# Weight pieces split 80 places further ahead in the scheduler's priority

## The chip, the cores and the metric

The kernel runs as one program on one core of a Trainium2 chip. The metric is device time in microseconds (us) of one execution, lower is better. Every number below comes from timed runs or from one execution recorded by the hardware profiler. Engines are named as the profile names them: PE (TensorE, matmuls), PEld (TensorE's weight loads), DVE (VectorE), ACT (ScalarE), POOL (GpSimd), SP (SyncE, which issues most transfers).

## The reference, cut to what matters

Two models of two layers each run one after the other on 256 tokens of width 1024, in float32. The first has an even layer (an mLSTM branch and a sparse-attention branch, "nsa", beside each other) and an odd layer (HGRN2, a gated linear recurrence). The second has, per layer, a mixer (pooling in layer 0, a gated unit "SGU" in layer 1) and an MLP, with gains and shifts that come from a conditioning vector ("ada").

```
x = x + even_layer(rms_norm(x) ...)       # mLSTM || nsa, then @ ev_w_out
x = x + hgrn2_layer(rms_norm(x) ...)      # then @ od_w_out
for i in range(2):
    mod = silu(c) @ ada_w[i] + ada_b[i]   # six vectors of 1024
    x = x + g1 * mixer_i(modulate(rmsnorm(x), sh1, sc1))
    x = x + g2 * (square(relu(modulate(rmsnorm(x), sh2, sc2) @ w1[i])) @ w2[i])
```

Most of the work is products of 256 tokens with large weight matrices.

## The kernel before, in words

**Weights.** Every large matrix is read in loads of 128 x 2048 numbers (1 MB) into one of three "raw" buffers (`load_raw`, line 150, issued by SP). A load holds two pieces of 128 x 1024. To keep float32 accuracy on the faster matmul form, a piece w is split into two parts (`split_w`, line 155): ACT copies w into a rounded buffer `whi` (line 161), DVE subtracts and writes the rest into `wlo` (line 162). There are four buffers of each. The activations are split in the same way into `ahi` and `alo` (or `ghl` for the MLP's hidden values). A product is then three matmuls per 128 x 128 block: whi with ahi, whi with alo, wlo with ahi (lines 221 to 223; lines 206 to 208 where the tokens are the stationary side; lines 1057 and 1058 in the MLP's second product, where one matmul takes ahi and alo together).

One piece makes one output tile: 24 matmuls for a piece of 8 blocks (`tile_T`), 12 or 24 in `tiles_tok`, 16 in the MLP's second product, where four pieces make one output tile. `Weights.piece` (line 181) asks for the load of a raw buffer when its first piece comes, and calls `split_w` just ahead of the tile's matmuls. The very first piece is split in halves (`ahead`, line 177), and its load comes in parts over ACT's queue (line 175): two halves of the first piece, then the whole second one.

**Order.** The kernel's text doesn't fix each engine's order. A scheduler does, when the program is built: every instruction gets a number as the text is traced, one more than the last; in a model of the chip, an engine that is free takes, of the instructions whose inputs and buffers are ready, the one with the lowest number. The order that results is then fixed for each engine's queue, and on the chip each engine follows it, waiting where something isn't ready yet. `tc.high_priority(offset=n)` lowers the numbers of the instructions inside by n. The kernel before uses it once: the modulation steps ("ada", line 340, DVE line 353: one product of 128 x 1024 and its sum, one load each, 96 in all) stand in a generator that `step` (line 373) advances with offset=-50, that is 50 places later. `pace` and `finish` call `step` so that the results are there when a layer needs them.

**Stages in time**, by the profile: the even layer's 35 column tiles with nsa and mLSTM between them (0 to 184 us; columns kc, vc, ks, kw, four nq, G, sv, v come first, then the preparation of nsa and mLSTM, then v, mq0, mk0 and so on), its output product (to 210), HGRN2 (to 345), pooling (to 372), MLP 0's first product (to 463) and second product (to 555), the SGU (to 630), MLP 1 (to the end). The result of a tile leaves PSUM over DVE (line 312) and, depending on the layer, over ACT and DVE again; three PSUM banks serve these tiles.

The start (lines 1153 to 1168) loads x in four parts, makes the first layer's operands (`operand`, lines 280 and 281: eight copies on ACT, eight subtractions on DVE), splits the first piece after the second operand, and squares x for the norm.

Of the kernel before, what the change touches and what calls it, by code (L numbers as in the profile page):

```python
# [65 lines left out]
def tile_kernel(ctx: ExitStack, tc: tile.TileContext, io: dict, out: bass.AP):  # L66
    nc = tc.nc
    V, S, G, PE = nc.vector, nc.scalar, nc.gpsimd, nc.tensor
    count = [0]

    def mk(pool, shape, dtype=F32, tag=None, bufs=None):
        count[0] += 1
        kw = {} if bufs is None else {"bufs": bufs}
        return pool.tile(list(shape), dtype, tag=tag or f"t{count[0]}", name=f"{tag or 't'}_{count[0]}", **kw)
# [80 lines left out]
    def split_w(raw, piece, halves=False):  # L155

        hi = mk(wpool, [128, 1024], F32R, "whi", bufs=4)
        lo = mk(wpool, [128, 1024], F32R, "wlo", bufs=4)
        r = raw[:, piece * 1024 : (piece + 1) * 1024]
        for c in [slice(0, 1024)] if not halves else [slice(0, 512), slice(512, 1024)]:  # L160
            S.copy(hi[:, c], r[:, c])  # L161
            V.tensor_sub(lo[:, c], r[:, c], hi[:, c])  # L162
        return hi, lo

    class Weights:
# [15 lines left out]
        def piece(self, i, n, halves=False):  # L181
            if i in self.split:
                return self.split.pop(i)
            c = i // 2
            if c not in self.raw:
                self.raw = {c: load_raw(self.src(c))}
            hi, lo = split_w(self.raw[c], i % 2, halves)
            return [w.rearrange("p (k n) -> p k n", n=n) for w in (hi, lo)]
# [1183 lines left out]
```

## Time and profile before

| | us |
|---|---|
| median of 3 runs | 825.5 |
| lowest, highest | 823.37, 827.38 |
| the profiled execution, as timed | 825.35 |
| its span, first to last instruction | 823.5 |
| TensorE (PE) busy in the span | 802.5 (97%) |
| VectorE (DVE) busy | 670.8 (81%) |
| ScalarE (ACT) busy | 519.7 (63%) |
| GpSimd (POOL) busy | 4.9 (1%) |
| mean granted TensorE clock | 0.990 |

How to read it: a matmul's busy time overlaps that of the next one, so a busy PE isn't PE at its peak; the count of matmuls in a stretch says more. In a row of the timeline the columns are start, duration, engine, line, operation, output <- inputs, shapes and count, and in brackets the idle time before it with what ended it. A row of waits gives who waited for whom, the total, how often and the longest. The granted clock is a share of TensorE's full speed.

### The profile page before, as it was taken

The numbers are of one execution on the slowest core, as the hardware profiler recorded it, in microseconds if no ns is written. First come the engines' busy times: TensorE is split into PE (matmuls) and PEld (weight loads), VectorE is DVE, ScalarE is ACT, GpSimd is POOL, SyncE is SP. The second block draws the span as 40 slices with busy tenths as digits, with TensorE's granted clock in tenths as the row PEclk, the third lists the DMA queues.
The fourth block names the chain that finished last, engine by engine and source line by source line (L and its number), as shares of the span: only waits on it lengthen the run. The fifth ranks groups of instructions, "written<-read, shape, count | busy, mean of one in ns | idle before, by whom it ended". The sixth has DMA issues, their size and how long they took to land.

```text
span 823.5 us, 16419 instructions
## 1 busy us (share of the span) xinstructions
PE 802.5 (97%) x6568; PEld 739.9 (90%) x6568; DVE 670.8 (81%) x1260; ACT 519.7 (63%) x932; POOL 4.9 (1%) x19
## 2 busy tenths in 40 slices
PE   8999999998999999998999999999999999999996
PEld 7969987888999987998999988889999999988885
DVE  7689988899999999998999988756679877755552
ACT  6656765686876565756877734446657877754441
POOL 0000000001000000000000000000000000000000
PEclk8999999999999999999999999999999999999999
DMA  9644566657885677747989888654446655555521
GB/s 353 244 165 148 179 215 229 228 191 258 301 288 214 245 253 262 232 174 284 345 283 320 304 294 310 245 201 154 168 152 234 221 199 166 193 190 174 199 103 52
DMA packets 34636, 184.66 MB, mean 224 GB/s; under 512 B 3968, under 2 KB 4608, under 8 KB 19200
## 3 DMA queue, kind: packets, MB, share of 16 engines
q1 hardware_dynamic: 33696, 181.96, 62.8%
q10 hardware_dynamic: 864, 1.65, 0.6%
q8 instruction: 52, 0.85, 0.4%
q14 instruction: 24, 0.20, 0.1%
HBM read 182.55 MB, written 1.05 MB: 223 GB/s over the span
## 4 chain that ended last, share of the span: by engine, by line
PE 68%; DVE 15%; DMA 8%; ACT 4%; issue 4%; ACTq 0%; DVEq 0%; SPq 0%
PE g L221 13%; PE g L223 12%; PE g L222 12%; PE g L1057 10%; DMA araw<-in_ada_w_dram 7%; DVE wlo L162 5%; PE g L1058 5%; DVE araw L353 3%; PE m L871 1%; ACT whi L161 1%; PE m L761 1%; DVE nt L312 1%; PE g L207 1%; PE g L208 1%; PE g L206 1%
## 5 line engine op out<-in xcount | busy, mean ns | idle before, releaser
L221 PE MATMUL g<-ahi,whi 128*128 128x258 f32 (+1 forms) x1256 | 359.3, 288 | 8.1 <-ACT ahi L213 3.3
L222 PE MATMUL g<-alo,whi 128*128 128x258 f32 (+1 forms) x1256 | 357.5, 286 | 0.1
L223 PE MATMUL g<-ahi,wlo 128*128 128x258 f32 (+1 forms) x1256 | 356.7, 285 | 0.3 <-DVE wlo L162 0.2
L162 DVE TENSOR_TENSOR wlo<-raw,whi 128x1024 fp32r<-128x1024 f32 (+1 forms) x238 | 288.7, 1216 | 79.9 <-ACT whi L161 79.2
L161 ACT CAST whi<-raw 128x1024 fp32r<-128x1024 f32 (+1 forms) x238 | 246.5, 1043 | 166.8 <-PE g L222 67.0
L221 PEld LDWEIGHTS g<-ahi,whi 128*128 128x128 f32 x1256 | 238.7, 191 | 12.7 <-ACT ahi L213 4.1
L222 PEld LDWEIGHTS g<-alo,whi 128*128 128x128 f32 x1256 | 240.0, 191 | 2.1 <-issue 0.8
L223 PEld LDWEIGHTS g<-ahi,wlo 128*128 128x128 f32 x1256 | 239.3, 191 | 2.1 <-issue 1.0
L1057 PE MATMUL g<-ghl,whi 128*128 128x512 f32 x480 | 168.2, 393 | 0.0
L353 DVE CUSTOM_DVE_ANT_0 araw<-araw,row_c,prm 128x1024 f32<-128x1024 f32 x96 | 122.4, 1278 | 18.0 <-DMA araw<-in_ada_w_dram 17.9
L1058 PE MATMUL g<-ghl,wlo 128*128 128x256 f32 x480 | 134.1, 279 | 0.6 <-DVE wlo L162 0.6
L1057 PEld LDWEIGHTS g<-ghl,whi 128*128 128x128 f32 x480 | 89.9, 187 | 21.2
L1058 PEld LDWEIGHTS g<-ghl,wlo 128*128 128x128 f32 x480 | 89.9, 187 | 1.2 <-DVE wlo L162 1.2
L312 DVE TENSOR_TENSOR nt<-g,nrstd 128x256 f32<-128x256 f32 x133 | 55.5, 418 | 15.1 <-PE g L223 14.3
L1039 ACT ACTIVATE nt<-nt,nb 128x256 f32<-128x256 f32 x64 | 32.4, 507 | 23.5 <-DVE nb L1038 23.5
L280 ACT ACTIVATE ahi<-xT,gains 128x256 fp32r<-128x256 f32 x32 | 16.2, 505 | 23.6 <-DVE xT L332 22.2
L286 ACT ACTIVATE sq<-xT 128x256 f32<-128x256 f32 x56 | 22.3, 404 | 10.6 <-DVE xT L332 10.6
L214 DVE TENSOR_TENSOR ghl<-nt,ghl 128x256 fp32r<-128x256 f32 x64 | 26.9, 422 | 2.2 <-ACT ghl L213 0.2
L1040 ACT ACTIVATE nt<-nt 128x256 f32<-128x256 f32 x64 | 26.7, 418 | 1.9
L213 ACT CAST ghl<-nt 128x256 fp32r<-128x256 f32 x64 | 25.9, 406 | 1.8
L208 PE MATMUL g<-wlo,ahi 128*128 128x512 f32 (+1 forms) x64 | 24.3, 379 | 0.0
L206 PE MATMUL g<-whi,ahi 128*128 128x512 f32 (+1 forms) x64 | 24.2, 378 | 0.0
(302 smaller groups left out, 803.1 us busy)
## 6 DMA issues: line engine op xcount, KB each, us to landing
raw<-in_mlp_w_dram SPq DMA_DIRECT2D x64, 1024.0 KB, 5.0
araw<-in_ada_w_dram SPq DMA_DIRECT2D x96, 512.0 KB, 4.9
raw<-in_ev_w_in_dram SPq DMA_DIRECT2D x17, 1024.0 KB, 5.5
raw<-in_od_w_in_dram SPq DMA_DIRECT2D x16, 1024.0 KB, 5.2
raw<-in_sgu_w_in_dram SPq DMA_DIRECT2D x8, 1024.0 KB, 4.9
raw<-in_ev_w_out_dram SPq DMA_DIRECT2D x4, 1024.0 KB, 4.9
raw<-in_od_w_out_dram SPq DMA_DIRECT2D x4, 1024.0 KB, 4.8
raw<-in_sgu_w_out_dram SPq DMA_DIRECT2D x4, 1024.0 KB, 4.8
```

The lines of the kernel that those rows point to most:

```text
L161: S.copy(hi[:, c], r[:, c])
L162: V.tensor_sub(lo[:, c], r[:, c], hi[:, c])
L206: PE.matmul(ps[tb], pair.hi(k)[:, ts_], wh[:, j, :], start=st, stop=False)
L208: PE.matmul(ps[tb], pair.hi(k)[:, ts_], wl[:, j, :], start=False, stop=sp)
L221: PE.matmul(ps, wh(k), ah(k), start=st, stop=False)
L222: PE.matmul(ps, wh(k), al(k), start=False, stop=False)
L223: PE.matmul(ps, wl(k), ah(k), start=False, stop=sp)
L312: V.tensor_tensor(t, ps[:, :T], self.r, op=ALU.mult)
L353: V.tensor_tensor_reduce(raw, raw, crow, 1.0, P("ada_b", layer * 48 + c), ALU.mult, ALU.add, mod[:, c : c + 1])
L1039: S.activation(r, r, AF.Relu, bias=b)
L1057: PE.matmul(ps, wh[:, k, :], a.rearrange("p s t -> p (s t)"), start=st, stop=sp, skip_group_check=True)
L1058: PE.matmul(ps[:, :T], wl[:, k, :], a[:, 0, :], start=False, stop=sp, skip_group_check=True)
```

## The change

The copy and the subtraction of `split_w` get numbers lower by 80. The load of the raw buffer, the matmuls and the modulation steps keep theirs. Nothing else is changed: the same instructions, buffers and sizes.

```diff
@@ -157,9 +157,11 @@
         hi = mk(wpool, [128, 1024], F32R, "whi", bufs=4)
         lo = mk(wpool, [128, 1024], F32R, "wlo", bufs=4)
         r = raw[:, piece * 1024 : (piece + 1) * 1024]
-        for c in [slice(0, 1024)] if not halves else [slice(0, 512), slice(512, 1024)]:
-            S.copy(hi[:, c], r[:, c])
-            V.tensor_sub(lo[:, c], r[:, c], hi[:, c])
+
+        with tc.high_priority(offset=80):
+            for c in [slice(0, 1024)] if not halves else [slice(0, 512), slice(512, 1024)]:
+                S.copy(hi[:, c], r[:, c])
+                V.tensor_sub(lo[:, c], r[:, c], hi[:, c])
         return hi, lo
```

## Rows read from the trace of the kernel before

**Rows 1.** The page, part 1: busy us, share of the span, instructions.

```profile
PE 802.5 (97%) x6568; PEld 739.9 (90%) x6568; DVE 670.8 (81%) x1260; ACT 519.7 (63%) x932; POOL 4.9 (1%) x19
```

**Rows 2.** Busy by stretch: start:end, length, PE, PEld, DVE, ACT, POOL, clock, DMA.

```profile
8.36:14.50 6.14, 6.01 (x25) 5.44 (x26) 5.76 (x15) 6.14 (x13) 0.00 (x0) 0.50 1.00 420
75.40:80.00 4.60, 4.55 (x26) 4.40 (x25) 4.13 (x10) 2.14 (x7) 0.20 (x2) 0.63 0.63 228
...
184.00:196.00 12.00, 8.95 (x67) 8.13 (x67) 10.70 (x27) 6.30 (x13) 2.71 (x2) 1.00 0.70 232
...
380.00:460.00 80.00, 80.00 (x658) 79.04 (x657) 77.45 (x159) 58.92 (x106) 0.00 (x0) 1.00 0.86 307
460.00:500.00 40.00, 40.00 (x239) 35.35 (x238) 35.10 (x56) 22.34 (x34) 0.00 (x0) 1.00 0.84 301
500.00:520.00 20.00, 19.41 (x109) 16.50 (x109) 17.20 (x26) 7.81 (x12) 0.00 (x0) 1.00 0.81 280
640.00:720.00 80.00, 80.00 (x667) 80.00 (x667) 61.08 (x116) 63.73 (x112) 0.00 (x0) 1.00 0.56 193
```

**Rows 3.** Line 162 (the subtraction): which weight loads waited for it (us, times).

```profile
  PEld g L1058: 1.2, 2
  PEld g L223: 0.9, 3
```

**Rows 4.** Waits, ACT: waiter <- releaser: us in total, times, longest us.

```profile
ACT whi L161 <- PE g L222: 67.0, 73, 3.8
ACT whi L161 <- PE g L1057: 62.6, 44, 1.8
```

**Rows 5.** Groups by line and shape: busy us, mean ns, idle before.

```profile
L162 DVE TENSOR_TENSOR wlo<-raw,whi 128x1024 fp32r<-128x1024 f32 x236 | 287.4, 1220 | 78.0 <-ACT whi L161 77.3
L161 ACT CAST whi<-raw 128x1024 fp32r<-128x1024 f32 x236 | 245.3, 1047 | 165.0 <-PE g L222 67.0 <-PE g L1057 62.6 <-PE g L207 12.1
...
L353 DVE CUSTOM_DVE_ANT_0 araw<-araw,row_c,prm 128x1024 f32<-128x1024 f32 x96 | 122.4, 1278 | 18.0 <-DMA araw<-in_ada_w_dram 17.9
```

**Rows 6.** Timeline of DVE, then of PE, 502 to 507 us.

```profile
502.14 1.28 DVE L353 CUSTOM_DVE_ANT_0 araw<-araw,row_c,prm 128x1024 f32<-128x1024 f32 x1 [1.21 <-DMA araw<-in_ada_w_dram]
...
503.49 1.28 DVE L353 CUSTOM_DVE_ANT_0 araw<-araw,row_c,prm 128x1024 f32<-128x1024 f32 x1
...
505.10 1.22 DVE L162 TENSOR_TENSOR wlo<-raw,whi 128x1024 fp32r<-128x1024 f32 x1
...
506.37 0.39 PE L1058 MATMUL g<-ghl,wlo 128*128 128x256 f32 x1 [0.59 <-DVE wlo L162]
```

**Rows 7.** Timeline of ACT, DVE and PE, 62 to 76 us: one split (mk0).

```profile
62.15 1.05 ACT L161 CAST whi<-raw 128x1024 fp32r<-128x1024 f32 x1 [4.08 <-PE g L207]
...
74.44 1.20 DVE L162 TENSOR_TENSOR wlo<-raw,whi 128x1024 fp32r<-128x1024 f32 x1
...
75.70 0.38 PE L223 MATMUL g<-ahi,wlo 128*128 128x256 f32 x1
```

**Rows 8.** Timeline of ACT, 0 to 12 us, and landing of line 175's three transfers.

```profile
1.17 1.42 ACTq L175 DMA_DIRECT2D raw<-in_ev_w_dram  x3
...
7.28 0.62 ACT L161 CAST whi<-raw 128x512 fp32r<-128x512 f32 x1 [1.66 <-DMA raw<-in_ev_w_dram]
7.81 2.50 ACT L280 ACTIVATE ahi<-xT,norm_w 128x256 fp32r<-128x256 f32 x6
...
DMA to landing us min/median/max: 3.8/5.6/7.0
```

**Rows 9.** Waits of SyncE's queue.

```profile
SPq L152 <- DVE wlo L162: 380.7, 99, 10.0
SPq L352 <- DVE mod L353: 108.0, 41, 7.9
```

**Rows 10.** Timeline of ACT, 174 to 176 us.

```profile
174.84 1.05 ACT L161 CAST whi<-raw 128x1024 fp32r<-128x1024 f32 x1 [2.21 <-PE g L222]
175.80 0.46 ACT L766 ACTIVATE A<-m,nnmx 128x256 f32<-128x256 f32 x1
```

## The prediction

> **What bounds the kernel now.** I read the page first, then the busy time by stretch, then who waits for whom, and only then the order on single engines. The page has TensorE busy for 802.5 of 823.5 us [rows 1]. The stretches say how much of that is work: in the second MLP's first product TensorE issues 667 matmuls in 80 us, 120 ns each, without a gap, while VectorE is busy for 61 and ScalarE for 64 of the 80 us [rows 2]. That is TensorE's own pace. The first MLP's first product, where VectorE is nearly full (77.45 of 80 us), still gets 658 in 80 us, 9 fewer or 1.1 us [rows 2], and the SGU's preparation (line 1090) has its matmuls in this stretch, so none of it is put down to splits. So in the long stretches TensorE is the bound and a split that comes earlier has nothing to give. It can give only where TensorE stands still for a split.
>
> That sum is small. Weight loads waited for the low part of a piece 1.2 us in two cases and 0.9 us in three [rows 3]; matmul rows of the same stalls are not counted twice. The other direction is much larger: ScalarE, having reached a split, stood 67.0 us in 73 cases and 62.6 us in 44 cases until TensorE gave back the buffer of the piece four before [rows 4]. Of 238 rounding copies at least 117 were therefore at the head of their queue before their buffer was free. A higher priority can't move those: four buffers set their time.
>
> **The change, part by part.** Nothing is added or removed: 238 copies of mostly 1.047 us on ScalarE and 238 subtractions of mostly 1.220 us on VectorE stay [rows 5]; their place in the two queues moves. 80 places are, counted in the code, some 2.4 tiles of the first MLP product (24 matmuls, 2 split, 6 for the result, without the modulation steps), or four pieces of the second (16 matmuls and 2). Since a split can't start before the piece four before it is done, it is ready 3 to 4 tiles before its own place. So in the first product the results of that older tile still come first; what the split now passes is mostly a modulation product (line 353, 1.278 us on VectorE [rows 5]), whose own number is raised by 50. In the second product the split passes all of them.
>
> *Second product of the first MLP.* The row to read is the subtraction at 505.10 us: ahead of it stand two modulation products, the first held 1.21 us for its own transfer, and TensorE waits for the subtraction until 506.37 us [rows 6]. From 460 to 500 us TensorE issues 239 matmuls in 40 us, from 500 to 520 us 109 in 20 us, where 119.5 are due if the mix is the same; the second stretch also holds no other wait on a split than these two, 1.2 us by the waits [rows 2, 3]. With the split first they go: **-1.2 us**. The modulation product comes one or two subtractions later (1.2 to 2.4 us); the steps that the next layer needs are issued several pieces earlier than their use, so I cost that at nothing. If that cover is gone, the next layer's first operands are late by those 2.4 us at most, once.
>
> *Columns mq0 and mk0 of the even layer.* The copy of one piece begins at 62.15 us, its subtraction only at 74.44 us, and TensorE takes up the low part at 75.70 us, as soon as it is there [rows 7]. This split stands 91 places behind the start of its group of columns, so after the change 11 behind it: it passes the evictions of v and mq0, not the preparation of the attention. That is enough for the 0.3 us of wait. Of the three cases of 0.9 us in all, one is this, one is the second tile, and one is the very first, which waits for the transfer and stays: two thirds, **-0.6 us**. From 75.4 to 80 us the granted clock is 0.63, between the levels of 1.2 and 2.4 GHz [rows 2]; at full clock the stretch would be 4.60 x 0.37 = 1.7 us shorter. Whether an earlier split keeps the clock up no row tells; bounds 0 and -1.7 us. I take 0, because the wait that ends there is too short to be the whole cause, and keep 1.7 us for the range.
>
> *The start.* The second tile's split, 69 places behind the first operand, comes ahead of them by 11 after the change; only the first split stands before it. Its transfer is the last of three issued from 1.17 us on, one each 0.47 us, and the slowest of the three lands 7.0 us after its issue, near 9.1 us if it is the third [rows 8]. ScalarE runs operands two to seven from 7.81 us on for 2.5 us. If the split is put ahead of all of them, they start at 9.1 + 1.05 = 10.2 us, 2.4 us late; if behind three of them, TensorE hardly notices, since it takes 0.74 us an operand at the granted clock of 0.50 that it has there, the 1.2 GHz level (25 matmuls in 6.14 us, three an operand) [rows 2], where ScalarE makes one in 0.42 us. Bounds: -0.5 us (the second tile no longer waits, which is already counted above) and +2.4 us. I take **+0.3 us**: the row of 7.28 us shows that ScalarE's order put a copy ahead of data that came 1.66 us later, and the order behind it is likely to mix.
>
> *Queues.* The loads keep their number, but each raw buffer comes free with its second subtraction: SyncE waits 380.7 us in 99 cases for subtractions, and 108.0 us in 41 cases for modulation products [rows 9]. Earlier subtractions bring weight loads forward; later modulation products hold the queue for the weight load behind them. The two offset each other, with the loads' wait the larger; cost 0, and cover is the three raw buffers. GpSimd holds no instruction of the split and nothing on it is passed.
>
> Sum: -1.2 - 0.6 + 0.3 = -1.5 us. The profiled execution took 825.35 us (its span 823.5 us and 1.85 us around it), 0.15 us under the median of 825.5. So **823.9 us**. What the measurement of this kernel can tell from no change is about 0.5%, 4.1 us.
>
> **Rivals.** *It does nothing.* For it: the 117 copies that already wait for their buffer [rows 4]. Against it: 121 that do not, and the subtractions that come 11 us behind their copy [rows 7]. Time 825.4 us.
>
> *It gives more.* VectorE is the engine whose order changes most, and two places where TensorE is short of work hang on it: the stretch at low clock (1.7 us) and the end of the attention, where TensorE is busy for 8.95 of 12 us between 184 and 196 us [rows 2], 3.05 us idle. If splits done earlier leave VectorE free there, the sum is -1.8 - 1.7 - 3.05 = -6.6 us, 818.8 us. Against: at 184 us what is missing are results of the attention, not weights.
>
> *It is slower.* A split that is put further ahead and isn't ready holds whatever stands behind it. The profile has one such case: the copy at 174.84 us held ScalarE 2.21 us for TensorE, and the exponential of the attention's last block, next in the queue, started at 175.80 us [rows 10]. The price is 2.2 us a hold at the end of the attention, where TensorE has no other work, plus 2.4 us if the start goes wrong: 4.6 us, 830.0 us. It decides as soon as one more hold falls behind 160 us and the start is hit as well. The Trainium skill, "TensorE: Matmul & The Clock Gate", section on the array's 16 sub-arrays, has ScalarE's and VectorE's queues as strictly first in, first out, which speaks against moving a waiting instruction ahead; the trace agrees, as the exponential did not pass the waiting copy. Without such holds the rule costs nothing.
>
> **How the numbers follow.** Small gain 0.34, nothing 0.13, more 0.31, slower 0.22. The first two lie within 0.5%: 0.47. The forecast is the likeliest case's, whose own range is 821.5 to 826. The range goes to 816.5 (the larger gain and 2 us of reordering that I can't place) and to 830.5 (both holds).
>
> **What would show it.** Right: in 500 to 520 us the matmul count rises to about 115; the waits for the low part fall from five cases to one; subtractions follow their copies within 3 us even in 60 to 150 us, and modulation products come later. Wrong: TensorE's rows at 100 to 184 us shift by more than 2 us, the idle time of 184 to 196 us grows, ScalarE's operands at the start begin after 9 us, or the copies' waits for TensorE rise well above the 129.6 us of now [rows 4] with an attention step behind them.

## The result, and the profile after

The changed kernel takes 831.57 us (median of 14 runs, 828.18 to 836.62) where the kernel before takes 825.32 us (median of 14, 823.37 to 828.35): a ratio of 1.0065, 95% interval 1.005 to 1.0081. The ratios and intervals here and below are taken from all the runs of both kernels and differ a little from the quotient of the medians (here 1.0076). That is 4 to 7 us slower, where 1.5 us less had been forecast, and 1.1 us above the top of the range. The profiled execution of the changed kernel took 828.18 us, the lowest of its 14, with a span of 826.4 us; the two traces thus show 2.9 us of the 6.25 us between the medians. Lines moved by two: the copy is now line 163, the subtraction 164, the operands 282, the table's load 390, the product's three matmuls 223 to 225.

Page of the changed kernel, part 1, against [rows 1]:

```profile
PE 798.4 (97%) x6568; PEld 736.0 (89%) x6568; DVE 670.3 (81%) x1260; ACT 521.6 (63%) x933; POOL 4.8 (1%) x19
```

ScalarE has one instruction more, 933 for 932, though the diff adds none. Its place is in the timeline of ScalarE at the start (start, duration, engine, line, operation, operands, count, idle time before it):

```profile
2.62 1.28 ACT L163 ACT_TABLE_LOAD   x1 [2.62 <-issue]
4.90 0.62 ACT L163 CAST whi<-raw 128x512 fp32r<-128x512 f32 x1 [1.00 <-DMA raw<-in_ev_w_dram]
6.57 0.62 ACT L163 CAST whi<-raw 128x512 fp32r<-128x512 f32 x1 [1.05 <-DMA raw<-in_ev_w_dram]
8.64 1.04 ACT L163 CAST whi<-raw 128x1024 fp32r<-128x1024 f32 x1 [1.45 <-DMA raw<-in_ev_w_dram]
9.70 1.28 ACT L390 ACT_TABLE_LOAD   x1
11.00 3.30 ACT L282 ACTIVATE ahi<-xT,norm_w 128x256 fp32r<-128x256 f32 x8
...
23.58 0.47 ACT L395 ACTIVATE nrstd<-m,eps 128x256 f32<-128x256 f32 x1 [0.69 <-PE m L298]
```

The same engine in the kernel before, in part ahead of [rows 8]:

```profile
3.91 0.91 ACT L280 ACTIVATE ahi<-xT,norm_w 128x256 fp32r<-128x256 f32 x2
5.00 0.62 ACT L161 CAST whi<-raw 128x512 fp32r<-128x512 f32 x1 [0.18 <-DMA raw<-in_ev_w_dram]
...
18.89 0.47 ACT L393 ACTIVATE nrstd<-m,eps 128x256 f32<-128x256 f32 x1 [0.98 <-PE m L296]
```

Before, the first two operands began at 3.91 us and the other six at 7.81 us [rows 8]. Now all eight begin at 11.00 us. The 7.09 us of the first operand add up: three waits for transfers (1.00 + 1.05 + 1.45 = 3.50 us), three copies (0.62 + 0.62 + 1.04 = 2.28 us) and a second load of a function table (1.28 us), 7.06 us. Before there was one table load, the kernel's own preload at line 388, the first instruction of all; now two half copies and a whole one stand ahead of it, and they bring a load of their own. The last operand comes less late than the first, at 14.30 us for 10.31, 3.99 us: the two half copies and 0.18 + 1.66 = 1.84 us of waiting stood ahead of it before, too. New ahead of it are 1.66 us more of waiting, the whole copy (1.04 us) and the second table load (1.28 us), 3.98 us.

What TensorE waited for from 0 to 40 us (waiter, releaser, us in total, times, longest):

```profile
PE g L223 <- ACT ahi L282: 6.6, 1, 6.6
PE m L307 <- ACT nrstd L395: 1.1, 1, 1.1
```

The same 40 us by windows, first the kernel before, then the changed kernel with the stretches of [rows 2] (start:end, length, PE, PEld, DVE, ACT, POOL busy with counts, clock, DMA share, GB/s):

```profile
0.00:40.00 40.00, 36.60 (x259) 35.33 (x260) 28.51 (x53) 27.15 (x47) 1.01 (x10) 0.91 0.77 295
20.00:25.00 5.00, 5.00 (x44) 5.00 (x44) 4.16 (x12) 4.53 (x10) 0.00 (x0) 1.00 0.99 411
```

```profile
0.00:40.00 40.00, 30.80 (x209) 29.71 (x210) 25.92 (x49) 27.55 (x46) 1.01 (x10) 0.87 0.73 266
20.00:25.00 5.00, 3.45 (x22) 2.56 (x21) 4.21 (x9) 2.90 (x7) 0.00 (x0) 1.00 0.93 352
25.00:30.00 5.00, 4.99 (x29) 4.99 (x30) 3.18 (x8) 4.55 (x9) 0.00 (x0) 0.66 0.28 108
...
75.40:80.00 4.60, 4.23 (x36) 3.97 (x35) 4.48 (x15) 1.89 (x3) 0.00 (x0) 1.00 0.46 183
184.00:196.00 12.00, 9.97 (x82) 9.05 (x81) 11.49 (x26) 7.00 (x16) 0.00 (x0) 1.00 0.71 248
380.00:460.00 80.00, 78.66 (x644) 77.73 (x645) 76.36 (x159) 60.56 (x111) 0.00 (x0) 1.00 0.90 326
500.00:520.00 20.00, 19.86 (x115) 17.13 (x114) 17.21 (x27) 7.45 (x10) 0.00 (x0) 1.00 0.85 289
```

Fifty matmuls fewer in the first 40 us. At the full clock of 2.4 GHz one takes 0.118 us here (170 in the 20 us from 20 to 40 us in the kernel before), so this is 5.9 us, about the whole loss. The late operands cost TensorE time twice. The chain that ended last, cut to the part behind the first tile (start, duration, engine, what), shows the second time:

```profile
21.93 0.38 DVE sq L292
22.35 1.15 PE m L298 x4
23.58 0.48 ACT nrstd L395
24.09 0.42 ACT nrstd L395
```

The squares for the norm stand behind the operands. The norm's root was at 18.89 us before, now at 23.58 us; results of tiles leave PSUM multiplied by it (line 314), so nothing frees the three banks before that. From 20 to 25 us TensorE is busy 3.45 of 5 us and issues 22 matmuls, where it issued 44; behind this gap the granted clock is 0.66 from 25 to 30 us, between the levels of 1.2 and 2.4 GHz, where it was 1.00 in the kernel before. The loss doesn't need that fall. The second profiled execution of the changed kernel, the first of the experiments below, has 1.00 from 20 to 40 us (152 matmuls there, for 135 here) and lost no less; it was at the lower level before that instead, with a mean of 0.74 from 0 to 20 us (0.83 here). The kernel before has such a stretch as well, 0.50 from 8.36 to 14.50 us [rows 2]. Further on TensorE's pace is the old one: 668 matmuls for 667 from 640 to 720 us, in the second MLP. The 644 for 658 from 380 to 460 us go with a wait for VectorE's `nb` that both kernels have: of 2.2 us, up to 376.47 us, in the kernel before, and of 2.4 us, up to 381.35 us and so partly in this stretch, in the changed one.

Not all of the 5.9 us is left in this execution: the attention's last matmul comes at 187.24 us instead of 183.74, 3.5 us late, and the end 2.9 us late. This is the fastest of the 14 executions, and no trace of the first 14 shows where the slower ones lose the rest, up to the 6.25 us between the medians.

Of the forecast's signs, 500 to 520 us has the 115 matmuls that were expected. The subtraction's waiters, answering to [rows 3], over the whole span:

```profile
  PEld g L225: 1.4, 1
  PE g L225: 1.2, 1
  PEld g L1060: 0.9, 2
```

Five waits became three, but their sum stays: 1.4 + 0.9 = 2.3 us of weight loads against 1.2 + 0.9 = 2.1 us. The split of mk0 [rows 7] and the place of the new longest wait, in the timeline:

```profile
67.54 1.05 ACT L163 CAST whi<-raw 128x1024 fp32r<-128x1024 f32 x1 [3.85 <-PE g L209]
...
71.84 1.22 DVE L164 TENSOR_TENSOR wlo<-raw,whi 128x1024 fp32r<-128x1024 f32 x1
...
86.63 1.22 DVE L164 TENSOR_TENSOR wlo<-raw,whi 128x1024 fp32r<-128x1024 f32 x1
...
87.90 0.39 PE L225 MATMUL g<-ahi,wlo 128*128 128x256 f32 x1 [1.22 <-DVE wlo L164]
```

mk0's subtraction follows its copy by 4.3 us instead of 12.3. The piece two further on keeps its long gap: copy at 68.88 us and subtraction at 80.58 us before, 73.93 and 86.63 us now, and now TensorE waits for it. This wait comes with the order: the weight loads' 1.4 us stand at this piece in each of the five traces in which the even layer's splits are raised, and from 75 to 110 us the other seven have 0 to 1.2 us in at most two cases. Copies waiting for their buffer, against [rows 4]: 64.2 us in 76 cases (line 224) and 65.7 us in 46 (line 1059), together 129.9 us against 129.6: what waited for a buffer waits as before. In the order of the two engines' queues (counting the instructions that aren't splits or table loads ahead of each) only 42 of 238 copies and 94 of 238 subtractions changed place at all. In the first MLP's second product it is 2 of 32 copies and 10 of 32 subtractions, by one or two places; in the second MLP's second product none. Of the forecast's signs of being wrong, two came: operands after 9 us (11.00) and a shift of more than 2 us between 100 and 184 us (3.5). The idle time from 184 to 196 us didn't grow, and the copies' waits didn't rise.

### The profile page after: what moved, and what is told of

It reads as the page before. It is cut to its first block, busy times and chain, and to the rows that moved or that the text cites. A ratio compares the mean times of both kernels' runs of the same rounds, so it can differ in the third digit from the quotient of the medians.

```text
span 826.4 us, 16435 instructions
## 1 busy us (share of the span) xinstructions
PE 798.4 (97%) x6568; PEld 736.0 (89%) x6568; DVE 670.3 (81%) x1260; ACT 521.6 (63%) x933; POOL 4.8 (1%) x19
## 3 DMA queue, kind: packets, MB, share of 16 engines
HBM read 182.55 MB, written 1.05 MB: 222 GB/s over the span
## 4 chain that ended last, share of the span: by engine, by line
PE 64%; DVE 19%; DMA 8%; issue 4%; ACT 3%; ACTq 0%; DVEq 0%; SPq 0%
PE g L223 13%; PE g L224 12%; PE g L225 12%; PE g L1059 9%; DMA araw<-in_ada_w_dram 8%; DVE wlo L164 6%; PE g L1060 5%; DVE araw L355 4%; PE m L873 2%; DVE nt L314 1%; ACT whi L163 1%; PE g L209 1%; PE g L210 1%; PE g L208 1%; DVE ghl L216 1%
## 5 line engine op out<-in xcount | busy, mean ns | idle before, releaser
L163 ACT CAST whi<-raw 128x1024 fp32r<-128x1024 f32 (+1 forms) x238 | 247.1, 1043 | 164.9 <-PE g L1059 65.7
```

## The experiments

The theory after this reading: the start alone carries the loss, because the operands of the first layer, and behind them its norm, wait for transfers of weights. The rival: splits raised further on (the attention, the HGRN layer, the MLPs) hold other steps and carry part of it. Most kernels limit the raise to some pieces, counted in the order in which they are asked for (1 to 4 the start, 5 to 43 the rest of the even layer, 86 to 149 the first MLP; `pieces` starts at [0], and CONDITION stands for the limit):

```diff
-        with tc.high_priority(offset=80):
+        pieces[0] += 1
+        with tc.high_priority(offset=80) if CONDITION else nullcontext():
```

**The changed kernel again**, no edit.

> The changed kernel once more, with a second profile, on the chip of the next three. Both theories: 830 to 833 us. Theory S (the start alone): the profile shows TensorE idle from about 5 to 11.5 us and again near 24.5 us, as in the first profile of the changed kernel, and what differs between the two profiles further on is only at which stalls the granted clock falls. Theory R (the attention stretch, 30 to 184 us): pieces 15 to 35 fall behind those of the kernel before by more than they already are at piece 3.

Measured: 832.61 us (6 runs), the kernel before 825.27 us, ratio 1.0086 [1.0066, 1.0106]. The loss is there again.

**Raised from the fifth piece on**, CONDITION `pieces[0] > 4`.

> The raised priority only from the fifth piece on; the four pieces of the start keep their own. S: as fast as the kernel before or a little faster, 823.5 to 825.5 us, with the first operand on ScalarE near 3.9 us again. R: 829 to 831 us, since all that is moved in the attention stretch is still moved.

Measured: 825.85 us (12 runs), ratio 1.001 [0.9991, 1.0028]. Without the start, no loss clear of noise is left, at most 0.28% or 2.3 us; nor is there a gain. The theory's range was 823.5 to 825.5, the median lies 0.35 us above it.

**Raised for the first four pieces alone**, CONDITION `pieces[0] <= 4`.

> The raised priority for the first four pieces alone. S: 830 to 833 us, all of the loss. R: 825 to 828 us, the start's loss being mostly made up later.

Measured: 830.5 us (6 runs), ratio 1.0062 [1.0044, 1.0081]. Four of 238 pieces carry all or nearly all of it: 0.62% of 825.27 is 5.1 us. Whether the other 234 add a little is open, since the intervals of the two kernels overlap.

**The changed kernel with its table loaded first**:

```diff
-    tab[0] = Table(EXP_LN)
+    with tc.high_priority(offset=200):
+        tab[0] = Table(EXP_LN)
```

> The changed kernel, but the load of the exponential table is itself raised by 200, so that it stands ahead of the first split and ScalarE loads one table at the start, not two. S: the second load took 1.28 us in front of the eight operands, so 829.5 to 830.5 us, 1.3 us under the changed kernel. R: no difference from the changed kernel beyond 0.5 us.

Measured: 829.67 us (5 runs), ratio 1.0055 [1.0036, 1.0074]. ScalarE at the start:

```profile
9.25 1.04 ACT L163 CAST whi<-raw 128x1024 fp32r<-128x1024 f32 x1 [1.30 <-DMA raw<-in_ev_w_dram]
10.20 3.30 ACT L282 ACTIVATE ahi<-xT,norm_w 128x256 fp32r<-128x256 f32 x8
...
24.08 0.47 ACT L395 ACTIVATE nrstd<-m,eps 128x256 f32<-128x256 f32 x1 [2.25 <-PE m L298]
```

The second load is gone and the operands begin at 10.20 us instead of 11.00, with the transfer of the second piece 0.6 us later in this run. Yet the norm is no earlier, 24.08 us: its matmul stands in TensorE's queue behind the first three tiles, which run without a gap from 12.00 to 22.93 us; the granted clock is 0.50 up to 17.70 us in this execution, for 14.80 us in the first one of the changed kernel. The ratio is 0.3% below that of the changed kernel beside it, but the intervals overlap; the load alone is not settled by this pair.

**The first piece alone**, CONDITION `pieces[0] == 1`, and **the second piece alone**, `pieces[0] == 2`. These tell whether the late end of the operands counts or TensorE's late start.

> Only the split of the very first piece keeps the lowered numbers. Its two half copies and the second table load stand ahead of the eight operands, the second piece's copy stays where it was before. By the trace of after the second half's copy ends near 7.2 us and a table load takes 1.28 us, so the operands begin near 8.5 us (8.64 us would be a wait for the second piece, which is not there). Theory 'what counts is when the last of the eight operands is there' (8.5 + 8 x 0.42 = 11.9 us; before 10.3, changed kernel 14.4 us at +6 us): about 2 us, 827 to 828. Rival 'what counts is when TensorE starts' (before 5.67, after 11.56 us; here near 9.1): more than half of the loss, 829 to 830.

> Only the split of the second piece keeps the lowered numbers. One table load; two operands, half a copy of the first piece, then the second piece's copy, which waits for its transfer until about 8.6 us, and behind it the other half copy and operands three to eight, from about 10.3 us on. Theory 'last of the eight operands' (10.3 + 2.5 = 12.8 us; before 10.3, changed kernel 14.4 us at +6 us): 3 to 4.5 us, 828.5 to 830. Rival 'when TensorE starts': TensorE starts at 5.67 us as before, so at most 1 us, 825 to 826.5.

Measured: the first piece 827.35 us, ratio 1.0031 [1.0012, 1.0051]; the second 828.12 us, ratio 1.0044 [1.003, 1.0059]; the kernel before beside them 824.97 us. ScalarE with the first piece raised:

```profile
6.68 0.62 ACT L165 CAST whi<-raw 128x512 fp32r<-128x512 f32 x1 [0.81 <-DMA raw<-in_ev_w_dram]
7.32 1.28 ACT L392 ACT_TABLE_LOAD   x1
8.61 3.30 ACT L284 ACTIVATE ahi<-xT,norm_w 128x256 fp32r<-128x256 f32 x8
```

and with the second raised:

```profile
5.30 0.62 ACT L165 CAST whi<-raw 128x512 fp32r<-128x512 f32 x1 [0.41 <-DMA raw<-in_ev_w_dram]
8.70 1.56 ACT L165 CAST whi<-raw 128x1024 fp32r<-128x1024 f32 x2 [2.78 <-DMA raw<-in_ev_w_dram]
10.16 2.50 ACT L284 ACTIVATE ahi<-xT,norm_w 128x256 fp32r<-128x256 f32 x6
```

With the second piece raised TensorE's first tile starts at 5.97 us, nearly as before (5.67), and yet at least 0.3% is lost, 2.5 us, where the rival allowed 1 us; with the first piece TensorE starts only at 9.17 us, and no more is lost. So TensorE's start is not what counts. The time, 828.12 us, lies 0.4 us under the theory's range. One copy that waits 2.78 us for its transfer, ahead of half a copy and six operands, costs about as much as the first piece's two half copies and second table load; the two intervals overlap, so which is the larger is open. The two add up: 0.31 + 0.44 = 0.75%, against 0.62% for the start and 0.65% and 0.86% for the whole change.

**The even layer without its start**, CONDITION `4 < pieces[0] <= 43`, and **the first MLP alone**, `85 < pieces[0] <= 149`.

> The lowered numbers only for pieces 5 to 43, the even layer without its start. In the profiled run of the kernel with the start left out, this stretch was 2 to 3 us ahead of the kernel before from 76 to 210 us. If that is a gain that the later layers' raised splits gave back: 822.5 to 823.5 us. If it is the reordering of one run, or TensorE loses it again in later layers whatever their priorities: 825 to 826.5 us.

> The lowered numbers only for pieces 86 to 149, the first MLP. The forecast's term for this layer alone is -1.2 us: matmuls issued from 500 to 520 us rise from 109 to about 115, no wait for the low part there, and the time is 824.1 us (interval of the ratio below 1.000). Rival: the raised splits push the modulation product and later steps back by as much, the count rises in this stretch and falls in another: 825.3 us or a little more.

Measured: the even layer 824.87 us, ratio 1.0008 [0.9992, 1.0024]; the first MLP 825.86 us, ratio 1.0016 [1.0002, 1.003]. No gain in the even layer, although 28 of its 39 subtractions change place, up to 26 places. In the first MLP, where the forecast's largest term was, there is none either; if anything a small loss. Why the term isn't there is seen in the run that raised only the even layer. Its order of splits in the first MLP is that of the kernel before, place for place, and its row of 500 to 520 us is

```profile
500.00:520.00 20.00, 20.00 (x115) 17.42 (x115) 18.23 (x26) 9.09 (x13) 0.00 (x0) 1.00 0.80 275
```

115 matmuls and no wait, with nothing moved. VectorE there, to be held against [rows 6]:

```profile
504.95 1.28 DVE L357 CUSTOM_DVE_ANT_0 araw<-araw,row_c,prm 128x1024 f32<-128x1024 f32 x1
506.16 1.22 DVE L166 TENSOR_TENSOR wlo<-raw,whi 128x1024 fp32r<-128x1024 f32 x1
```

A modulation product still stands ahead of the subtraction, but it had no transfer to wait for. Over all traces, the weight loads of the second product of the first MLP waited for subtractions 1.2 us (the kernel before), 0, 0, 0, 0, 0 and 1.9 us where the order there is the old one, and 0.9, 0, 0, 0.3 and 2.8 us where it is the new one. The stall comes and goes under either order; that the transfers make it is seen in the one case of [rows 6], where its row names one.

**The first piece raised, its table loaded first**: the two edits together.

> As the run with the first piece alone raised, but with the load of the function table issued first, so that there is one table load and not two. The copies of the two halves stand ahead of all eight operands, which begin at about 7.3 us and end near 10.6 us (before: 10.3; first piece alone raised: 11.9). If the second table load was what the first piece's split cost: 825 to 826 us with a kernel before of 825, at least 1.3 us under the run with the first piece alone raised. Rival 'the copies' own waits for their transfers are the cost': 827 to 828 as there.

Measured: 826.52 us, the kernel before beside it 826.47 us, ratio 1.0009 [0.9989, 1.0028].

```profile
4.93 0.62 ACT L165 CAST whi<-raw 128x512 fp32r<-128x512 f32 x1 [1.02 <-DMA raw<-in_ev_w_dram]
7.52 0.62 ACT L165 CAST whi<-raw 128x512 fp32r<-128x512 f32 x1 [1.98 <-DMA raw<-in_ev_w_dram]
8.04 3.30 ACT L284 ACTIVATE ahi<-xT,norm_w 128x256 fp32r<-128x256 f32 x8
```

Here the half copies wait 3.00 us ahead of all eight operands, and no loss clear of noise is left (at most 0.28%): the last operand ends at 11.34 us against 10.31 us before. 0.31% fell to 0.09% with the second table load taken out. With the pair of the whole change that is twice the same direction, 0.2 to 0.3% or some 2 us, each time with intervals that overlap. The pair here was measured on two chips, each kernel against the kernel before on its own, and it differs in more than the table: with the first piece alone raised, the seventh piece's copy also moved, ten operations forward, to 21.86 us, where it waits 0.56 us for its buffer ahead of ScalarE's work on the first tiles' results; with the table first it keeps its old place.

**One step the other way**, in the kernel before: the second half of the first piece, for which ScalarE waited 1.66 us [rows 8], put behind the seventh operand:

```diff
-            S.copy(hi[:, c], r[:, c])
-            V.tensor_sub(lo[:, c], r[:, c], hi[:, c])
+            with tc.high_priority(offset=-9) if c.start == 512 else nullcontext():
+                S.copy(hi[:, c], r[:, c])
+                V.tensor_sub(lo[:, c], r[:, c], hi[:, c])
```

> The kernel before with one step moved the other way: the split of the first piece's second half, whose copy waits 1.66 us for its transfer ahead of six ready operands, gets numbers higher by 9, so that it stands behind the seventh operand. The operands run from 5.6 us on instead of 7.81, the half's copy at about 7.7 us, the last operand ends near 8.8 us instead of 10.3. If the time goes with the last operand: 1.5 us less, 823 to 824 us against a kernel before of 825. Rival 'only what passes more than its own slack counts, and the start has some': no difference.

Measured: 826.56 us, ratio 0.9992 [0.9966, 1.0019]: no difference. It did not test the theory, since the next limit came at once:

```profile
8.54 0.51 ACT L281 ACTIVATE ahi<-xT,norm_w 128x256 fp32r<-128x256 f32 x1 [0.75 <-DMA xT<-in_xT_dram]
8.96 0.60 ACT L162 CAST whi<-raw 128x512 fp32r<-128x512 f32 x1
9.47 0.51 ACT L281 ACTIVATE ahi<-xT,norm_w 128x256 fp32r<-128x256 f32 x1
```

The seventh operand waits for x itself until 8.54 us, so the last one ends at 9.98 us, only 0.33 us earlier than before. In this execution the start was already near what the arrival of x allows. The interval is also too wide, 0.27% or 2.2 us to either side, to show the 1.5 us that were expected.

The start in all runs, from each one's trace (end of the last operand, begin of the norm's root, matmuls issued from 0 to 40 us):

| raised | operands end | norm | matmuls | ratio |
|---|---|---|---|---|
| nothing (before) | 10.31 | 18.89 | 259 | 1 |
| one half 9 later | 9.98 | 18.68 | 261 | 0.9992 |
| even layer | 9.55 | 17.77 | 269 | 1.0008 |
| first MLP | 10.04 | 18.25 | 265 | 1.0016 |
| all but the start | 10.94 | 19.14 | 257 | 1.001 |
| first piece, table first | 11.34 | 19.55 | 254 | 1.0009 |
| first piece | 11.91 | 20.38 | 247 | 1.0031 |
| second piece | 12.66 | 21.39 | 240 | 1.0044 |
| all, table first | 13.50 | 24.08 | 218 | 1.0055 |
| first four pieces | 14.32 | 23.59 | 220 | 1.0062 |
| all (changed kernel) | 14.30 | 23.58 | 209 | 1.0065 |
| all, again | 14.19 | 24.06 | 216 | 1.0086 |

Five rows have the start's order of the kernel before or nearly so, and spread over 1.4 us at the operands and 12 matmuls (1.4 us), with ratios that can't be told from 1 or, for the first MLP, hardly. From there on the ratio follows the first three columns: the second piece has 19 matmuls fewer than the kernel before, 2.2 us by 0.118 us each, and lost 3.6 us (0.44%); the first four pieces 39, 4.6 us, and lost 5.1 us. A few matmul records can be missing in a trace, and where the lower clock falls differs between executions, so a count is good to some units only.

## Why the prediction was wrong

**The start** is the step that failed. The forecast took +0.3 us between bounds of -0.5 and +2.4 us; the first four pieces alone measure +5.1 us. It had the place, the mechanism (a copy that waits for its transfer ahead of operands that are ready) and even the sign by which it would show, operands that begin after 9 us. What it got wrong is what the splits pass. It counted the second piece against the six operands of 7.81 us and left the first piece where it was. But the first piece stands behind the second operand, and 80 places take it past all that is there: the two operands that had run at 3.91 us, and the table's load. So three waits of together 3.50 us stood ahead of all eight operands, and not one ahead of six, and with them a second table load of 1.28 us that no step of the forecast has. The third transfer itself came a little earlier than estimated, 8.64 us for 9.1. The last operand was 3.99 us late, where the forecast's worst case has 2.4. Then it priced the delay by TensorE's pace in the first tile alone, and stopped there: the norm behind the operands, 4.69 us late, and the three PSUM banks behind the norm are not in the sum.

It also chose badly between its bounds. It took a value near the lower one because the order "is likely to mix", while the row it named for that [rows 8] had ScalarE's order put a copy ahead of data that came 1.66 us later. That row spoke for the upper bound. The strict order of the queues, from the Trainium skill, "TensorE: Matmul & The Clock Gate", section on the array's 16 sub-arrays, was cited in the slower rival and agrees: no operand passed the three waiting copies.

**The second product of the first MLP**, -1.2 us. The count rose to 115 as forecast, and this proves nothing, because a kernel with the old order there issues 115 too. The step read one execution's stall as the order's doing. [rows 6] said it themselves: the first of the two modulation products was held 1.21 us for its own transfer. The size was read too high as well: 1.2 us is what the weight loads waited, and TensorE's own matmul stood still for 0.59 us [rows 6], all that the row of 500 to 520 us has idle (19.41 of 20 us busy [rows 2]). The claim that in the second product the split passes all results was wrong as well; 10 of 32 subtractions moved, by one or two places.

**Columns mq0 and mk0**, -0.6 us. The split of mk0 came 8 us closer to its copy, and its wait, 0.2 us of the weight load in the trace, went. Another piece of the same stretch got a wait of 1.22 us at 87.90 us with the new order, which the step doesn't have. The sign that subtractions follow within 3 us failed: 4.3 us for mk0, 12.7 us for that piece. The measured gain of the even layer is none: at most 0.08% by its interval, 0.7 us, which doesn't exclude a term as small as this one.

**The clock from 75.4 to 80 us**, taken as 0. It was 1.00 in the changed kernel, for 0.63 before. From 60 to 80 us it is 1.00 also in the run that raised only the start, whose order there is the old one. That an earlier split keeps it up isn't shown; it may be one execution's affair.

**Queues**, taken as 0: SyncE's waits for subtractions fell from 380.7 to 340.4 us and those for modulation products from 108.0 to 101.7 us [rows 9], and the time shows nothing of it. **That most copies can't move** was right and went further than the forecast drew from it: 196 of 238 kept their place, though 94 of 238 subtractions did move, also without a gain.

**The slower rival** (0.22, 830.0 us) had the right side and came within 1.6 us of the time, with the wrong shares: 2.4 us for the start, which took 5.1, and 2.2 us for a hold at the end of the attention, of which there is no sign. With all but the start raised, the attention's last matmuls came at 181.51 us instead of 183.74 us in the traces, and the ratio was 1.001. That its sum came so near is luck. One slip in the range changes nothing: its lower end is 816.8 us by the forecast's own terms, not 816.5.

What stays open: the worth of the second table load (about 2 us in two pairs whose intervals overlap), and whether the small loss with the first MLP raised, 1.0016 [1.0002, 1.003], is one. No kernel tried beats the kernel before.

## What to carry to other kernels

A priority raised by a fixed number of places passes whatever stands within that distance, so at the start of a program, where inputs still arrive, count from the first instruction what is passed, and ask of each raised instruction when its data lands and what ready work is then behind it. A stall that one execution shows, with a transfer in its row, may not be there in the next; before it is booked as a gain, look whether the order or the transfer made it. Where copies wait for a free buffer, their priority moves little, here 42 of 238 copies; more buffers would be the thing to try first, which no run here did.

## What the runs showed of the hardware

A plain copy on ScalarE that comes ahead of the kernel's own table load brings a table load of its own, 1.28 us, and the preload behind it takes 1.28 us again (2.62 and 9.70 us in the changed kernel). The Trainium skill, "ScalarE: Activation LUTs", section on what ACT_TABLE_LOAD costs, gives 1283 ns for the load and about 1380 ns of drain at every switch to a different set. The load agrees with the trace. The drain isn't seen: the copy ends at 9.68 us, the load runs from 9.70 us, and the first operand starts at 11.00 us. Which set the copy's load brings no row tells, so this switch may not be to a different set.

The transfers of the start land at different times in different executions: the copy of the second half began at 6.57 us and 7.23 us in two executions of the changed kernel, at 7.33 us in the run with its table first and at 7.52 us in the one with the first piece raised and its table first, each time having waited for its data.
